# Prologue loads, joint transposes and split order of a two-layer trunk kernel

## The chip, the core and the metric

The kernel runs on one NeuronCore of a Trainium2 chip. The metric is device time per execution in microseconds (us): before the change the median of three runs was 945.95 us (945.51 to 946.14). Five engines work beside each other, each through its own instructions in order: TensorE (PE; its weight loads are listed apart as PEld), VectorE (DVE), ScalarE (ACT), GpSimd (POOL) and SyncE (SP, here only a queue that issues DMAs). An instruction that waits holds up all that stand behind it on its engine.

## The reference, cut to what matters

Two layers run over 256 tokens of width 1024. Each layer is a feed-forward half-step, a mixer with three kinds of heads, and a second feed-forward half-step, and each of the three is set between two RMS norms:

```
for l in range(DEPTH):                                  # DEPTH = 2
    f = swiglu(rmsnorm(h, pre1[l]), wg1[l], wu1[l], wd1[l]);  h = h + 0.5 * rmsnorm(f, post1[l])
    m = mixer(rmsnorm(h, premx[l]), w_in[l], ..., w_out[l]);  h = h + rmsnorm(m, postm[l])
    f = swiglu(rmsnorm(h, pre2[l]), wg2[l], wu2[l], wd2[l]);  h = h + 0.5 * rmsnorm(f, post2[l])

rmsnorm(x, g) = x * rsqrt(mean(x * x) + 1e-6) * g
swiglu(h, wg, wu, wd) = (silu(h @ wg) * (h @ wu)) @ wd      # 1024 -> 2816 -> 1024
```

The mixer projects the normed tokens by `w_in` (q, k, v, z, and the inputs of a state-space scan, a pooling and an attention), and `w_out` brings the heads' outputs back to width 1024.

## The kernel before, in words

**Tokens and weights.** The 256 tokens are two tiles of 128 (t = 0, 1). All weights, some 180 MB, pass through the core once. They come in units of 1 MB (128 partitions by 2048 floats) into four buffers `raw` (L72, on SP's queue), and each is split for the matmuls into a rounded part `hi` (ACT, L103) and the remainder `lo` (DVE, L104), in two or four pieces; five such pairs can be held (SPLIT_BUFS). A product is then three passes on PE: x_hi by w_hi, x_hi by w_lo, x_lo by w_hi. `W.pump` (L115) loads and splits as far ahead as the buffers allow, at the place in the program where it is called.

**One sub-layer's entrance.** `square_sum` (ACT, L226) makes the sums of squares of the two halves of a token tile, `rsqrt_sum` adds eps on DVE (L215), the second sum on ACT (L218) and takes the power -1/2 on POOL (L220); DVE scales the tile (L252) into `n` (the normed tile, two halves). `pre_turn` (L255) then transposes the eight 128x128 blocks on PE (L261) into two PSUM banks, and `split_into` writes them as `xT` hi (ACT, L209) and lo (DVE, L210). After a sub-layer `post` (L229) does the same with the output norm and adds to `h`.

**First products.** `ffn_first` (L397) makes the first 512 columns of gate and up for tile t by `mm_half` (L315, matmul line L324): two weight units for the gate bank, two for the up bank, 12 matmuls each; then `gate` applies silu (ACT, L392) and multiplies (DVE, L394). For t = 0 this stands first, then the transposes of tile 1 (`turned()`), then t = 1. The mixer's `first` (L566) does likewise with q and dt (L313, 24 matmuls of 264 columns) and with k and v.

**Quads and pairs.** Columns of the feed-forward come in groups. A pair (`ffn_pair`, L416) is plain. A quad (`ffn_quad`, L439) multiplies two tiles by two column groups with seven products in place of eight: left factors S1 to S4 are sums and differences of `xT` blocks (L276 to L293), right factors T1 to T4 are sums of weight units made on DVE in place (L102), and one unit is added from memory by an accumulating DMA that POOL issues (L108) after the second piece of T1. Between the products stand the down projections of the columns before (`mm_rows`, L341), for which `turn_h` (L406) transposes the hidden tile (L410) and splits it (L209, L210).

**Order.** A scheduler orders the instructions of each engine at build time, by the order of the code and by `tc.issue_after(ins)`, which keeps what a block issues behind `ins` on that engine. The prologue stands at L941 to L960; `later()` (L964) loads the constants and gains after the first quad.

## Time and profile before

| what | value |
|---|---|
| median of three runs | 945.95 us |
| profiled execution | 946.24 us, of which the span of the trace is 944.5 us |
| PE busy | 927.3 us (98%) |
| DVE busy | 789.1 us (84%) |
| ACT busy | 580.8 us (61%) |
| POOL busy | 34.9 us (4%) |
| DMA | 190.56 MB, mean 202 GB/s |

All times inside the trace count from the start of the span. "Busy" of PE is a sum over pipelined matmuls whose ends are modelled, so the gaps in which PE had nothing to start are read from the idle time that a row gives in brackets and from the distance between the starts of rows.

### The profile page before, as it was taken

The numbers are of one execution on the slowest core, as the hardware profiler recorded it, in microseconds if no ns is written. First come the engines' busy times: TensorE is split into PE (matmuls) and PEld (weight loads), VectorE is DVE, ScalarE is ACT, GpSimd is POOL, SyncE is SP. The second block draws the span as 40 slices with busy tenths as digits, with TensorE's granted clock in tenths as the row PEclk, the third lists the DMA queues.
The fourth block names the chain that finished last, engine by engine and source line by source line (L and its number), as shares of the span: only waits on it lengthen the run. The fifth ranks groups of instructions, "written<-read, shape, count | busy, mean of one in ns | idle before, by whom it ended". The sixth has DMA issues, their size and how long they took to land.

```text
span 944.5 us, 13133 instructions
## 1 busy us (share of the span) xinstructions
PE 927.3 (98%) x5058; PEld 792.5 (84%) x5058; DVE 789.1 (84%) x1067; ACT 580.8 (61%) x923; POOL 34.9 (4%) x47
## 2 busy tenths in 40 slices
PE   7999999999999999999999999999999999999997
PEld 4779898989888789898887888898898887989895
DVE  5899898589887998989499989876888799989872
ACT  5666656468737575747467656556694566656651
POOL 1000000010001000000010000000000010000000
PEclk9999999999999999999999999999999999999999
DMA  8757767555343476758463958583833263858531
GB/s 318 224 216 264 263 182 279 213 190 212 134 149 136 135 272 210 284 148 297 173 196 116 352 143 307 146 318 117 275 128 134 90 201 122 329 180 281 177 116 45
DMA packets 28004, 190.56 MB, mean 202 GB/s; under 512 B 3107, under 2 KB 3363, under 8 KB 5925
## 3 DMA queue, kind: packets, MB, share of 16 engines
q1 hardware_dynamic: 25920, 176.34, 51.0%
q0 software_dynamic: 1728, 12.58, 7.3%
q8 instruction: 40, 0.66, 0.3%
q10 hardware_dynamic: 292, 0.79, 0.2%
q14 instruction: 24, 0.19, 0.1%
HBM read 188.65 MB, written 1.05 MB: 201 GB/s over the span
## 4 chain that ended last, share of the span: by engine, by line
PE 85%; DVE 6%; ACT 5%; issue 2%; DMA 2%; POOL 0%; DVEq 0%; POOLq 0%; ACTq 0%
PE acc L341 26%; PE wk L435 22%; PE wk L305 21%; PE wk L324 10%; DVE lo L104 3%; ACT hi L103 3%; PE wk L410 1%; ACT n L226 1%; DMA raw<-in_ff_q 1%; DVE raw L102 1%; PE wk L873 1%; PE wk L261 1%; DMA n<-in_gains 1%; ACT xT L209 1%; POOL s L220 0%
## 5 line engine op out<-in xcount | busy, mean ns | idle before, releaser
L104 DVE TENSOR_TENSOR lo<-raw,hi 128x1024 fp32r<-128x1024 f32 (+2 forms) x440 | 468.1, 1101 | 58.5 <-ACT hi L103 57.5
L103 ACT ACTIVATE hi<-raw 128x1024 fp32r<-128x1024 f32 (+2 forms) x440 | 400.0, 959 | 167.3 <-DVE raw L102 45.4
L341 PE MATMUL acc<-hi,t 128*128 128x512 f32 x832 | 219.9, 394 | 1.8 <-ACT t L209 1.3
L341 PEld LDWEIGHTS acc<-hi,t 128*128 128x128 f32 x832 | 153.1, 188 | 36.4 <-ACT t L209 5.0
L305 PE MATMUL wk<-xT,hi 128*128 128x256 f32 x1088 | 143.5, 284 | 0.0
L305 PEld LDWEIGHTS wk<-xT,hi 128*128 128x128 f32 x1088 | 136.6, 191 | 1.6
L341 PE MATMUL acc<-lo,t 128*128 128x512 f32 x416 | 114.5, 390 | 0.0
L435 PE MATMUL wk<-hi,n 128*128 128x512 f32 x384 | 102.6, 390 | 1.2 <-DVE t L210 1.2
L324 PE MATMUL wk<-hi,xT 128*128 128x512 f32 x384 | 101.1, 396 | 1.8 <-ACT xT L209 1.0
L341 PEld LDWEIGHTS acc<-lo,t 128*128 128x128 f32 x416 | 78.1, 188 | 16.5
L102 DVE TENSOR_TENSOR raw<-raw,raw 128x1024 f32<-128x1024 f32 x72 | 86.1, 1216 | 3.4 <-DMA raw<-in_ff_q 3.4
L324 PEld LDWEIGHTS wk<-hi,xT 128*128 128x128 f32 x384 | 71.1, 189 | 18.9 <-ACT hi L103 2.2
L435 PEld LDWEIGHTS wk<-hi,n 128*128 128x128 f32 x384 | 71.8, 188 | 17.2 <-issue 2.4
L435 PE MATMUL wk<-hi,xT 128*128 128x512 f32 x288 | 77.8, 392 | 0.0
L305 PE MATMUL wk<-xT,lo 128*128 128x256 f32 x544 | 76.8, 283 | 0.0
L305 PEld LDWEIGHTS wk<-xT,lo 128*128 128x128 f32 x544 | 70.3, 192 | 0.0
L435 PEld LDWEIGHTS wk<-hi,xT 128*128 128x128 f32 x288 | 53.6, 188 | 11.5 <-DVE t L466 0.7
L209 ACT ACTIVATE t<-wk 128x256 fp32r<-128x256 f32 x72 | 26.8, 375 | 43.3 <-DVE t L210 22.1
L324 PE MATMUL wk<-lo,xT 128*128 128x512 f32 x192 | 52.6, 393 | 0.1
L435 PE MATMUL wk<-lo,n 128*128 128x512 f32 x192 | 51.5, 389 | 0.0
L234 DVE TENSOR_TENSOR n<-acc,gains 128x512 f32<-128x512 f32 x24 | 16.5, 687 | 35.8 <-ACT n L226 35.8
L324 PEld LDWEIGHTS wk<-lo,xT 128*128 128x128 f32 x192 | 35.9, 188 | 8.6 <-DVE lo L104 1.0
(172 smaller groups left out, 764.8 us busy)
## 6 DMA issues: line engine op xcount, KB each, us to landing
raw<-in_ff_q SPq DMA_DIRECT2D x48, 1024.0 KB, 5.0
raw<-in_ff_d SPq DMA_DIRECT2D x44, 1024.0 KB, 5.0
raw<-in_ff_f SPq DMA_DIRECT2D x16, 1024.0 KB, 6.0
raw<-in_ff_q POOLq DMA_DIRECT2D x12, 1024.0 KB, 8.0
raw<-in_ff_g SPq DMA_DIRECT2D x12, 1024.0 KB, 4.8
raw<-in_ff_u SPq DMA_DIRECT2D x12, 1024.0 KB, 4.9
raw<-in_w_in SPq DMA_DIRECT2D x10, 1024.0 KB, 4.9
raw<-in_w_kvz SPq DMA_DIRECT2D x8, 1024.0 KB, 5.2
```

The source lines that it names most:

```text
L102: nc.vector.tensor_tensor(raw[:, s], self.raw[x][:, s], self.raw[y][:, s], op=op)
L103: self.act = nc.scalar.activation(hi[:, s], raw[:, s], AF.Copy)
L104: nc.vector.tensor_tensor(lo[:, s], raw[:, s], hi[:, s].bitcast(F32), op=ALU.subtract)
L209: split_into.last = nc.scalar.activation(hi, src_f32, AF.Copy)
L226: nc.scalar.activation(junk, x, AF.Square, scale=1.0 / (gain * math.sqrt(n)), accum_out=ssq)
L234: nc.vector.tensor_tensor(fg[i], f[i], gains[:, 1, i * 512 : (i + 1) * 512], op=ALU.mult)
L261: nc.tensor.transpose(ps[:, k * P : (k + 1) * P], xn[i][:, k * P : (k + 1) * P], ident)
L305: nc.tensor.matmul(ps, w[:, k, s], y[:, k, :], start=i == 0 and k == 0, stop=i == 2 and k == KD - 1)
L324: m = nc.tensor.matmul(ps, y[:, k, :], w[:, k, :], start=h == 0 and n == 0, stop=h == 1 and n == len(parts) - 1)
L341: nc.tensor.matmul(acc[b], x[:, j, s], w[:, j, b * 512 : (b + 1) * 512], start=first and j == 0 and i == 0, stop=last and j == 1 and i == 2)
L410: nc.tensor.transpose(ps[:, k * P : (k + 1) * P], hf[:, k * P : (k + 1) * P], ident)
L435: nc.tensor.matmul(ps, x[:, k, :], w[:, k, :], start=first and n == 0, stop=n == len(parts) - 1, skip_group_check=not first)
```

## The change

**Prologue.** The first token tile and the two gain rows are issued on SP's queue ahead of the weights, not on ACT's queue beside them; the first weight unit comes in two transfers of half its size, and two of its four pieces are split before the transposes, not one. The copies of tile 0 that the quads need (`keep`) stand later on ACT. The constants, gains and the mixer's small parameters are loaded after the first pair, not the first quad, and the three casts of constants follow the splits of that place.

**Norms.** eps is added on POOL (L215 before, L219 after). In `post` both squares stand ahead of the scaled copies.

**Entrances.** `mm_half` takes an `ahead`, which it calls in the second weight unit before the last four of its twelve matmuls. The transposes of tile 1 stand there, in `ffn_first(0)` and in the mixer's `first(0)`, and no longer behind the whole product. Silu of the gate bank is issued as soon as that bank is done. In the program's first feed-forward the factors S1 and S2 (`middle`) are made after the products of `ffn_first(1)` and one further weight split, elsewhere straight after `ffn_first(0)`; the rest of the factors stands behind the splits of `turn_h`; the first weight unit of the first quad, and the mixer's second one (C), are split in four pieces; `pump` calls at the entrances hold one pair fewer and stand behind named instructions.

```diff
...
-    def pump(self):
+    def pump(self, most=SPLIT_BUFS):
...
                 self.load()
-            elif self.split < len(self.jobs) and self.held < SPLIT_BUFS and self.ready():
+            elif self.split < len(self.jobs) and self.held < most and self.ready():
                 self.split_next()
...
     h = consts.tile([P, NT, D], F32, name="h")
-    nc.scalar.dma_start(h[:, 0, :], a["x"][:P, :])
+    nc.sync.dma_start(h[:, 0, :], a["x"][:P, :])
     grow = [buf(tag="n"), buf(tag="n")]
...
         nc.vector.memset(grow[i], 0.0)
-        nc.scalar.dma_start(grow[i][:1], a["gains"][0, 0:1, i * 512 : (i + 1) * 512])
+        nc.sync.dma_start(grow[i][:1], a["gains"][0, 0:1, i * 512 : (i + 1) * 512])
     cst = consts.tile([P, C_ALL], F32, name="cst")
...
+    def cast_constants():
         nc.scalar.activation(after_r, after, AF.Copy)
...
         split_into.last = nc.scalar.activation(hi, src_f32, AF.Copy)
-        nc.vector.tensor_tensor(lo, src_f32, hi.bitcast(F32), op=ALU.subtract)
+        split_into.lower = nc.vector.tensor_tensor(lo, src_f32, hi.bitcast(F32), op=ALU.subtract)
...
         v, r = tiny(1), tiny(1)
-        nc.vector.tensor_scalar(v, ssq[0], eps, None, op0=ALU.add)
+        nc.gpsimd.tensor_scalar(v, ssq[0], eps, None, op0=ALU.add)
         for s in ssq[1:]:
             w = tiny(1)
-            nc.scalar.activation(w, s, AF.Identity, bias=v)
+            rsqrt_sum.last = nc.scalar.activation(w, s, AF.Identity, bias=v)
             v = w
...
+    def pump_behind(ins):
+        with tc.issue_after(ins.ins):
+            W.pump()
...
-        ssq = [square_sum(f[0], D, gain)]
+        ssq = [square_sum(f[i], D, gain) for i in range(2)]
+        r = rsqrt_sum(ssq, EPS / (gain * gain))
         scaled(0)
-        ssq.append(square_sum(f[1], D, gain))
-        r = rsqrt_sum(ssq, EPS / (gain * gain))
         scaled(1)
...
+        def middle():
+            part("S1", s1)
+            nc.vector.tensor_tensor(x11, s1, x11, op=ALU.subtract)
+            part("S2", x11)
...
         nc.vector.tensor_tensor(s1, turned[0], s1, op=ALU.subtract)
-        part("S1", s1)
         nc.vector.tensor_tensor(s3, x11, turned[0], op=ALU.subtract)
-        nc.vector.tensor_tensor(x11, s1, x11, op=ALU.subtract)
-        part("S2", x11)
-        left["rest"] = rest
+        left["middle"], left["rest"] = middle, rest
         for i, (name, k, t_) in enumerate((("X11", 0, 0), ("X12", 4, 0), ("X22", 4, 1))):
...
             for n, (k, i) in enumerate(parts):
+                if ahead and h == 1 and n == 8:
+                    ahead()
                 y, w = ((x[0], hi), (x[0], lo), (x[1], hi))[i]
...
                 g1, u1, u2 = (W.unit(src[k]) for k in (0, 1, 3))
-                p["g1", i] = W.job(g1)
+                p["g1", i] = W.job(g1, pieces=2 if i > QUADS[0] else 4)
                 p["T1", i] = W.job(g1, (g1, ALU.add, u1), then=(u1, src[3]))
...
-    def gate(pg, pu):
-        s = buf()
-        nc.scalar.activation(s, pg, AF.Silu)
+    def gate(pg, pu, s=None):
+        if s is None:
+            s = buf()
+            nc.scalar.activation(s, pg, AF.Silu)
         hf = buf()
...
-    def ffn_first(t, p, pin=False):
+    def ffn_first(t, p, pin=False, ahead=None, between=None):
...
         for i in range(2):
-            mm_half(ps[i], [p["f", i, k] for k in range(2)], t, pin)
-        hf = gate(*ps)
-        W.pump()
+            mm_half(ps[i], [p["f", i, k] for k in range(2)], t, pin, ahead if i else None)
+            if not i:
+                s = buf()
+                nc.scalar.activation(s, ps[0], AF.Silu)
+        hf = gate(*ps, s)
+        with tc.issue_after(pre_turn.lower.ins):
+            if between:
+                W.split_next()
+                between()
+            W.pump(SPLIT_BUFS - t)
         return hf
...
         turn(1)
-        W.pump()
         if "rest" in left:
-            left.pop("rest")()
+            with tc.issue_after(split_into.last.ins):
+                left.pop("rest")()
+                W.pump()
+        else:
+            W.pump()
         pb = bank()
...
         hT = {}
-        hf = [ffn_first(0, p, pin=later is not None)]
-        turned()
-        hf.append(ffn_first(1, p))
+        hf = [ffn_first(0, p, later is not None, turned)]
+        middle = left.pop("middle")
+        if later is None:
+            middle()
+        hf.append(ffn_first(1, p, between=middle if later else None))
...
                 before = [i, i + 1]
-            if later:
+            if later and i in PAIRS:
                 later()
...
         post(1, acc[1], gain)
+        summed = rsqrt_sum.last
         xn1 = before_next(1)
-        W.pump()
-        return lambda: pre_turn(1, xn1, left=next_left)
+        W.pump(SPLIT_BUFS - 1)
+        def turn_second():
+            pre_turn(1, xn1, left=next_left)
+            pump_behind(split_into.last)
+        if next_left is not None:
+            pump_behind(summed)
+            return lambda: pre_turn(1, xn1, left=next_left)
+        return turn_second
...
         for i, k in enumerate(("B", "C", "x0", "x1", "u")):
-            p[k] = W.plan(a["w_in"][l, i], pieces=2 if i else 4)
+            p[k] = W.plan(a["w_in"][l, i], pieces=2 if i > 1 else 4)
         for k in range(2):
...
-    def mixer(l, p, turned, next_left, before_next):
+    params = {}
+    def load_params(l):
         vec = small.tile([P, V_ALL], F32, tag="vec", name=f"vec{l}", bufs=1)
...
         nc.sync.dma_start(row, a["row"][l : l + 1, :].to_broadcast([P, R_ALL]))
+        return vec, row
+    def mixer(l, p, turned, next_left, before_next):
+        vec, row = params.pop(l) if l in params else load_params(l)
...
-        def first(t):
+        def first(t, ahead=None):
             pq, pkv = bank(), bank()
...
             last and W.done(p["q"])
-            mm_half(pkv, [p["kv", k] for k in range(2)], t)
             c = buf()
...
             nc.vector.tensor_tensor(dtr[:, t, :], pq[:, 256:QDT], row[:, R_DTB : R_DTB + HEADS], op=ALU.add)
+            mm_half(pkv, [p["kv", k] for k in range(2)], t, ahead=ahead)
             nc.scalar.activation(c[:, 256:], pkv[:, :256], AF.Copy)
...
-        first(0)
-        turned()
+        first(0, turned)
         first(1)
...
     left = {}
-    W.split_next((0,))
+    W.split_next((0, 1))
     keep = pre_turn(0, xn0, left=left, late=True)
     with tc.issue_after(split_into.last.ins):
-        W.split_next((1, 2, 3))
+        W.split_next((2, 3))
         W.load()
...
     with tc.issue_after(W.act.ins):
-        keep()
         W.split_next()
...
         xn1 = pre_scale(1, gain)
-        W.pump()
+        keep()
+        W.pump(SPLIT_BUFS - 1)
...
     def later():
-        more_constants()
-        load_gain(1, 0, 1)
-        load_gain(0, 0, 2)
+        with tc.issue_after(W.dma.ins):
+            more_constants()
+            load_gain(1, 0, 1)
+            load_gain(0, 0, 2)
+            params[0] = load_params(0)
+        with tc.issue_after(W.act.ins):
+            cast_constants()
...
```

The first place is SP's queue at the program's start; `h` is the token tile, `n` the two gain rows, `raw` the weight units. Before:

```order
L1086 UNCONDITIONAL_BRANCH
L78 DMA raw_105<-in_ff_f 128x2048
L78 DMA raw_107<-in_ff_f 128x2048
L942 DMA h<-in_x 128x1024
L78 DMA raw_154<-in_ff_f 128x2048
L78 DMA raw_156<-in_ff_f 128x2048
```

and after the change:

```order
L1132 UNCONDITIONAL_BRANCH
L166 DMA h<-in_x 128x1024
L170 DMA n_75<-in_gains 1x512
L170 DMA n_76<-in_gains 1x512
L78 DMA raw_105<-in_ff_f 128x1024 x2
L78 DMA raw_108<-in_ff_f 128x2048
L984 DMA h<-in_x 128x1024
L78 DMA raw_155<-in_ff_f 128x2048
L78 DMA raw_157<-in_ff_f 128x2048
```

Three small issues now stand ahead of the first weights on SP, and the first unit is two issues.

The second place is ACT in the first quad. `t_391` (after: `t_388`) and `t_393` (`t_390`) are the transposed hidden tile, from PE's banks `wk_395` and `wk_434` (`wk_392`, `wk_431`); `raw_200` (`raw_201`) is the unit to which the accumulating DMA (DMASW0) adds; names in square brackets are the semaphores an instruction waits for. Before:

```order
L103 ACTIVATE hi_375<-raw_214 128x1024
L209 ACTIVATE t_391<-wk_395 128x2x128 [waits PE_49]
L103 ACTIVATE hi_383<-raw_200 128x1024 [waits DMASW0_49,Activation_49]
L103 ACTIVATE hi_367<-raw_198 128x1024 [waits DVE_49]
L103 ACTIVATE hi_383<-raw_200 128x1024
L209 ACTIVATE t_391<-wk_434 128x2x128 [waits PE_49]
L209 ACTIVATE t_393<-wk_395 128x2x128 [waits DVE_49]
```

and after the change:

```order
L103 ACTIVATE hi_372<-raw_199 128x1024 [waits DVE_49]
L213 ACTIVATE t_388<-wk_431 128x2x128 [waits PE_49]
L213 ACTIVATE t_390<-wk_392 128x2x128 [waits DVE_49]
L213 ACTIVATE t_390<-wk_431 128x2x128 [waits DVE_49]
L213 ACTIVATE n_440<-t_280 128x512
L468 ACTIVATE t_414<-wk_401 128x512
L472 ACTIVATE t_429<-wk_416 128x512
L213 ACTIVATE n_445<-t_197 128x512 [waits DVE_49]
L103 ACTIVATE hi_449<-raw_201 128x1024 [waits DMASW0_49,Activation_49]
```

The split that waits for the accumulating DMA stood ahead of three of the four copies of the hidden tile; now it stands behind all four.

The third place is PE at the entrance of the first layer's second feed-forward; `n_2855`, `n_2856` (after: `n_2864`, `n_2865`) are the halves of the normed tile 1, and `hi`, `lo` the weight units. Before:

```order
L324 MATMUL wk_2904<-lo_2886,xT_103 128x512 x4
L324 MATMUL wk_2904<-hi_2885,xT_104 128x512 x4
L261 MATMUL wk_2957<-ident,n_2855 128x128 x4
L261 MATMUL wk_2964<-ident,n_2856 128x128 x4
L324 MATMUL wk_2985<-hi_2607,xT_103 128x512 x4
```

and after the change:

```order
L336 MATMUL wk_2917<-lo_2895,xT_103 128x512 x4
L268 MATMUL wk_2964<-ident,n_2864 128x128 x4
L268 MATMUL wk_2971<-ident,n_2865 128x128 x4
L336 MATMUL wk_2917<-hi_2894,xT_104 128x512 x4
L336 MATMUL wk_2998<-hi_2616,xT_103 128x512 x4
```

Four matmuls that stood ahead of the eight transposes now stand between them and the first product of tile 1, which reads what ACT makes of the transposes.

## Rows read from the trace of the kernel before

**Rows 1.** The page: engines over the span, and the chain that ended last.

```profile
PE 927.3 (98%) x5058; PEld 792.5 (84%) x5058; DVE 789.1 (84%) x1067; ACT 580.8 (61%) x923; POOL 34.9 (4%) x47
...
PE 85%; DVE 6%; ACT 5%; issue 2%; DMA 2%; POOL 0%; DVEq 0%; POOLq 0%; ACTq 0%
```

**Rows 2.** Timeline 0 to 17 us: start, us, engine, line, tile [idle before, releaser].

```profile
0.79 0.41 ACTq L165 DMA_DIRECT2D h<-in_x  x1
...
7.30 0.63 ACT L226 ACTIVATE n<-h 128x512 bf16<-128x512 f32 x1 [3.73 <-DMA h<-in_x]
...
7.64 3.75 PE L945 MATMUL acc<-n,n 128*128 128x512 f32 x4 [2.57 <-DMA n<-in_gains]
...
9.49 0.80 POOL L220 TENSOR_TENSOR s<-s,halfexp 128x1 f32<-128x1 f32 x1 [8.13 <-ACT s L218]
...
11.18 2.17 PE L261 MATMUL wk<-ident,n 128*128 128x128 f32 x8
...
13.00 0.78 PE L324 MATMUL wk<-hi,xT 128*128 128x512 f32 x1
...
14.55 1.54 PE L324 MATMUL wk<-hi,xT 128*128 128x512 f32 x3 [0.78 <-ACT hi L103]
```

**Rows 3.** DMA issues of the first 20 us: count, KB each, median us to landing.

```profile
raw<-in_ff_f SPq DMA_DIRECT2D x4, 1024.0 KB, 9.7
...
h<-in_x ACTq DMA_DIRECT2D x1, 512.0 KB, 6.5
```

**Rows 4.** DMA issues of the whole span: a transfer with the queues empty.

```profile
out<-h SPq DMA_DIRECT2D x3, 256.0 KB, 2.1
```

**Rows 5.** Timeline 26 to 40 us: ACT at tile 1, and the end of the first products.

```profile
26.08 1.28 ACT L392 ACT_TABLE_LOAD   x1
...
27.87 1.08 ACT L209 ACTIVATE xT<-wk 128x512 fp32r<-128x512 f32 x2
...
39.55 0.60 PE L410 MATMUL wk<-ident,t 128*128 128x128 f32 x4
...
39.91 1.17 PE L435 MATMUL wk<-hi,xT 128*128 128x512 f32 x4
```

**Rows 6.** The chain of waits, 35 to 48 us: start, us, what.

```profile
35.79 1.14 DVE raw L102
...
37.25 8.60 DMA raw<-in_ff_q
...
45.94 2.02 ACT hi L103 x2
```

**Rows 7.** Timeline 49 to 54 us: PE in the first quad.

```profile
49.21 1.21 PE L341 MATMUL acc<-hi,t 128*128 128x512 f32 x4 [1.27 <-ACT t L209]
...
51.86 1.88 PE L341 MATMUL acc<-hi,t 128*128 128x512 f32 x7 [0.52 <-DVE t L210]
```

**Rows 8.** Stretch: us, busy (count) of PE, PEld, DVE, ACT, POOL, clock, DMA share, GB/s.

```profile
54.00:200.00 146.00, 145.97 (x801) 127.06 (x801) 124.84 (x143) 92.01 (x128) 3.18 (x4) 1.00 0.66 228
```

**Rows 9.** Timeline 205 to 212 us: entrance of the first mixer.

```profile
205.38 1.41 DVE L252 SCALAR_TENSOR_TENSOR n<-h,s,gains 128x512 f32<-128x512 f32 x2 [0.44 <-POOL s L220]
...
206.81 1.04 PE L261 MATMUL wk<-ident,n 128*128 128x128 f32 x8
...
208.21 1.25 PE L313 MATMUL wk<-hi,xT 128*128 128x264 f32 x8 [0.36 <-ACT xT L209]
...
210.33 1.63 PE L313 MATMUL wk<-hi,xT 128*128 128x264 f32 x8
```

**Rows 10.** Timeline 305 to 331 us: entrance of the first layer's second feed-forward.

```profile
305.72 1.42 DVE L252 SCALAR_TENSOR_TENSOR n<-h,s,gains 128x512 f32<-128x512 f32 x2 [0.44 <-POOL s L220]
...
308.54 1.03 PE L261 MATMUL wk<-ident,n 128*128 128x128 f32 x8
...
309.83 1.19 PE L324 MATMUL wk<-hi,xT 128*128 128x512 f32 x4 [0.25 <-ACT xT L209]
...
330.57 1.17 PE L435 MATMUL wk<-hi,n 128*128 128x512 f32 x4 [0.39 <-DVE t L210]
```

**Rows 11.** Line L220 over the span: count: min/median/max ns, first and last start.

```profile
L220 POOL TENSOR_TENSOR s<-s,halfexp x28: 547/870/1437, 9.5 to 939.5; 128x1 f32<-128x1 f32 x28
```

More of the change, by code (lines that the diff above doesn't have):

```diff
@@ L77, in load @@
         for c in range(0, cols, step):
-            self.nc.sync.dma_start(t[:, c : c + step], src[:, c : c + step])
+            self.dma = self.nc.sync.dma_start(t[:, c : c + step], src[:, c : c + step])
         self.raw[i] = t
@@ L263, in pre_turn @@
             split_into(xT, at, ps.rearrange("p (k n) -> p k n", k=4))
+            pre_turn.lower = split_into.lower
             turned.append(ps)
@@ L313, in mm_tok, with mm_half @@
                 nc.tensor.matmul(ps, x[:, k, s], w[:, k, :], start=i == 0 and k == 0, stop=i == 2 and k == KD - 1)
-    def mm_half(ps, us, t, pin=False):
+    def mm_half(ps, us, t, pin=False, ahead=None):
         for h, u in enumerate(us):
@@ L931, in mixer @@
         post(1, acc[1], 1.0)
+        summed = rsqrt_sum.last
         xn1 = before_next(1)
-        W.pump()
+        W.pump(SPLIT_BUFS - 1)
+        pump_behind(summed)
         return lambda: pre_turn(1, xn1, left=next_left)
@@ L938, in hybrid_trunk_kernel @@
         plans.append((plan_ffn(l, 1), plan_mix(l), plan_ffn(l, 2)))
-    W.load()
+    W.load(2)
     W.load()
@@ L959, in hybrid_trunk_kernel @@
         xn1 = pre_scale(1, gain)
-        W.pump()
+        keep()
+        W.pump(SPLIT_BUFS - 1)
     turned = lambda: pre_turn(1, xn1, left=left)
     def later():
-        more_constants()
-        load_gain(1, 0, 1)
-        load_gain(0, 0, 2)
+        with tc.issue_after(W.dma.ins):
[5 more added lines that the diff above has]
+            cast_constants()
     for l in range(DEPTH):
```

## The prediction

> **What bounds the kernel now.** I read the page first. PE is busy 98% of the span and holds 85% of the chain that ended last [rows 1], so only time in which PE has nothing to start can be won. The stretches say where that is: from 54 to 200 us PE is busy 145.97 of 146 us, with the clock granted in full [rows 8]; the gaps lie in the first 54 us and at the five later entrances of a sub-layer. The timeline shows each gap's releaser. The profiled execution took 946.24 us, 1.7 us of it outside the span; I make the sum against it and take 0.3 us off at the end, since the median is 945.95.
>
> *Prologue.* PE's first product of weights starts at 13.00 [rows 2]. Back from there: transposes at 11.18, the power on POOL at 9.49, the first square at 7.30, and that one waited for the token tile, which ACT issued at 0.79 [rows 2] and which landed 6.5 us later, while the weight units beside it took 9.7 us [rows 3].
>
> *First products.* Three further matmuls wait for ACT's split, to 14.55 [rows 2]. At tile 1 ACT loads a table (1.28 us) and then writes xT, at 27.87 [rows 5]. The products end at 39.55.
>
> *First quad.* PE waits 1.27 us for a copy of the hidden tile on ACT and 0.52 us for its remainder on DVE [rows 7]. The chain shows why: the accumulating DMA ran from 37.25 to 45.85, and ACT's split that needs it (45.94) stands ahead of the copy [rows 6].
>
> *Entrances.* In the mixer the eight transposes start at 206.81 and the next product at 208.21 [rows 9]; in the feed-forward at 308.54 and 309.83 [rows 10]. Four transposes unhindered take 0.36 us from start to start (39.55 to 39.91) [rows 5], so eight take 0.72: the mixer loses 0.68 us, the feed-forward 0.57. The mixer's third pass (x_lo) takes 1.63 us against 1.25 for eight like it, 0.38 more [rows 9]; the quad loses 0.39 us at 330.57 [rows 10]. There are two mixers, and three feed-forwards beside the first, each like the one shown.
>
> **The change part by part.**
>
> *Loads in one queue.* Before, 512 KB of tokens shared the engines with the weights. Now they go first. Nearest rows: 256 KB through an empty queue landed 2.1 us after issue [rows 4]. Twice the bytes can take at most twice that, 4.2, and the part that does not grow with the bytes is in it once: I take 3.3 us, between the two, landing at 4.1 instead of 7.3. Bounds: 2.1 (half the size) and 6.5 (as now), that is a gain of 4.4 to 0 us. The chain behind it keeps its length except for two things: two splits (0.6 us each) stand on ACT ahead of the second sum, not one, +0.6; and the gain rows, which PE's broadcast product needs, come on the same queue ahead of the weights, so that product (3.75 us [rows 2], started at 7.64) moves up too. Against +0.6 stands the second scaled half, which before waited for that product. Gain 3.0 us. The price: three issues of some 0.4 us stand ahead of the first weights on SP, and two of them wait for memsets of VectorE, so every weight unit starts up to 1.6 us later. ACT did not reach the fourth unit's split until long after its landing, which hides that; uncovered it would cost 1.6 us.
>
> *Two pieces split early, later copies.* The wait of 14.55 less 13.00 less a matmul goes in part: two matmuls now have their weights, the third and fourth wait for splits behind xT. Of some 1.1 us I take 0.7; the saved copies and the silu ahead of its turn on ACT give 0.5 more at tile 1. Gain 1.2 us, bounds 0 and 2.5 (what these products lose beyond 96 unhindered matmuls, after the 1.1, is no more). What is late next is DVE's splits of the first quad.
>
> *First quad.* The copies now stand ahead of the split that waits for the DMA, and the constants (five transfers, 2 MB) no longer run in this stretch. Both sums of T1 come before the next factor on DVE, so the accumulation starts earlier. I take 1.27 + 0.52 = 1.8, and 0.2 for short waits beside them: gain 2.0 us. DVE then has ten splits and sums of 1.14 us, the first of [rows 6], between T1 and the hidden tile; by my sequence of its instructions the tile's remainder is ready about when PE asks. If it is late by one of them the gain is 0.8; bounds 0 and 2.5.
>
> *Constants after the first pair.* Nothing reads them before the first mixer or the output norm; the five transfers move past some twelve weight loads on SP. PE did not wait once from 54 to 200 [rows 8]: nothing.
>
> *Transposes ahead of the last four matmuls.* Four matmuls of 0.23 us cover ACT's two copies (0.6 us each) almost wholly. In the feed-forward the normed tile is ready at 305.72 + 1.42 = 307.14 and the transposes would stand at 308.54 - 0.91 = 307.63 [rows 10]: ready by 0.5 us, gain 0.57 of 0.57. In the mixer it is ready at 206.79 [rows 9] and the transposes would stand at 205.90, so PE waits 0.9 us, less what the shorter norm chain saves. In the old order ACT has a split between the last sum of `post` and its addition (1.0 us each, by the two of [rows 6]), and the new order has the addition on POOL instead: about 0.8. Then 0.1 to 0.2 is left. Gain 0.5 of 0.68, and 0.3 of the 0.38, since xT's remainder is made sooner too: 0.8 a mixer, bounds -0.3 and 1.2. For the feed-forwards I add half of the quad's 0.39 and 0.1 of small waits: 0.85 each, bounds 0 and 1.5.
>
> *eps on POOL.* 28 additions leave DVE, where a row stood in a queue behind other work. The power on POOL took 0.55 to 1.44 us [rows 11]; an addition of one column is not shown there. From above it is bounded by the slowest of these, 1.44, from below by nothing. I take 0.55, the power's fastest. With two sums the addition runs beside the second square (0.63 us [rows 2]) and costs nothing; four single sums in the mixers pay about 0.4 us each where the state-space result is not waited for. If the cover is gone, see the slower rival.
>
> *Four pieces for the first quad's unit and for C, fewer pairs held, silu with its bank.* Twelve splits become 24 of half size, under 0.1 us each on ACT and DVE, hidden by PE; one pair fewer held matters only where splits run just ahead of PE. Nothing.
>
> *Tail.* The last tile's chain has the same steps in the same order: nothing.
>
> Sum: 3.0 + 1.2 + 2.0 + 2 x 0.8 + 3 x 0.85 = 10.35 us. 946.24 - 10.35 = 935.9, and with the 0.3 us to the median 935.6; I round to **936**.
>
> One rule speaks against the addition on POOL. The slowest powers (1.44 us) come while DVE subtracts two SBUF tiles, the fastest (0.55) at the very end where DVE is idle [rows 11]. The Trainium skill ("SBUF — State Buffer", Who interferes with whom) says that a VectorE instruction with two SBUF inputs and a GpSimd instruction that reads SBUF exclude each other, and whichever comes second waits. By that rule, the trace agrees: 0.55 against 1.44.
>
> **Rivals.**
>
> *A: the entrances give nothing.* The normed tile is late and PE waits in front of the transposes as long as it waited behind them. For it: 0.9 us in the mixer. Against: 0.5 us to spare in the feed-forward. 945.95 - 6.2 = 939.8.
>
> *B: the start gives only the token tile's 3 us.* DVE's sums and splits set the first quad, so PE arrives early and waits. For it: DVE was busy 84% [rows 1] and the splits of the first quad were finished within a few us of their use. Against: ACT's split there waited for a DMA of 8.60 us [rows 6], which none of DVE's work did. 945.95 - 3.0 - 4.15 = 938.8.
>
> *C: hardly anything.* Weights bound the start, the token tile gains nothing, and the entrances fall short: 945 to 947. For it: the same bytes pass the same 16 engines. Against: no row of the start waits for a first weight unit.
>
> *D: slower, by the addition on POOL.* Each entrance has two roots in line on tile 1 (output norm, then input norm). If each addition waits for a DVE operation on two SBUF tiles of 1.14 us [rows 6] and then runs 0.87 (the power's median [rows 11]), it ends 2.0 us after the first sum, 1.4 us later than the second square (0.63): ten of them, 14 us, less 1.5 us to spare in three feed-forwards, and the entrances' gain is gone. 945.95 - 6.2 + 12.5 = 952.3, or 953.7 with one more at the start. It makes the kernel slower once an addition ends more than about 0.8 us after the second square, at 1.4 us length. Against: DVE's pieces at the entrances are mostly half size.
>
> **How the numbers follow.** My forecast 0.55; A 0.13; B 0.13; C 0.11; D 0.08. The forecast's own range from its terms is 932.5 to 938.5: the better bounds are 1.4 + 1.3 + 0.5 + 0.8 + 1.95 beyond the sum, of which I allow a bit over half together. A and B lie inside 942.5; C and D stay out. Range **932.5 to 942.5**. A measurement of this kernel tells no change from a change beyond about 0.2%, 1.9 us: faster is the forecast, A, B and a sliver of C and D, 0.85; within it the bulk of C, 0.08; slower most of D, 0.07.
>
> **What would show it.** Right: the first square near 4.1 us and the first weight product near 10; the product's end near 35; no wait of PE above 0.5 us in the first quad; transposes and next products at the entrances without an idle of PE between; the pair's first product some 6 us earlier than before. Wrong: a first square past 6; PE waiting for DVE's `lo` around 40 to 60 us; idle time of PE in front of the transposes; additions on POOL over a microsecond with the scalar addition on ACT behind them.

## The result and the profile after

The changed kernel takes 937.51 us (median of 5 runs, 937.19 to 937.75) where the kernel before takes 945.95 (945.51 to 946.14): ratio 0.9911, 95% interval 0.9896 to 0.9925. The profiled spans are 935.5 and 944.5 us. The page answers to [rows 1]: PE's busy time fell from 927.3 to 921.8 (waits hidden in stretched matmuls went), and PE's share of the chain rose from 85 to 94%.

```profile
PE 921.8 (99%) x5058; PEld 792.9 (85%) x5058; DVE 788.1 (84%) x1051; ACT 580.4 (62%) x935; POOL 41.4 (4%) x75
...
PE 94%; DVE 2%; ACT 1%; POOL 1%; issue 1%; DMA 1%; POOLq 0%; DVEq 0%; SPq 0%; ACTq 0%
```

Where the 9.0 us of span came from is read by comparing the start of the same PE instruction in both traces:

| PE instruction | before | after | gain so far |
|---|---|---|---|
| first product of weights | 13.00 | 12.47 | 0.53 |
| first transposes of a hidden tile (end of the first products) | 39.55 | 37.41 | 2.14 |
| transposes in the first pair (behind the first quad) | 78.60 | 74.06 | 4.54 |
| hidden tile, second feed-forward | 321.00 | 315.35 | 5.65 |
| hidden tile, third | 501.81 | 494.79 | 7.02 |
| hidden tile, fourth | 781.84 | 773.00 | 8.84 |

To give each place its own share I add up, over both traces, how much later each matmul's successor starts than at the unhindered pace (0.227 us for 512 columns, 0.121 for 264), and call it PE's loss; it counts equal work, whatever its order. By that: up to the first product 0.53, first products 1.61, first quad 2.40, mixers 0.52 each, later feed-forwards 1.35, 1.29 and 1.39 (entrance and quad), tail -0.54, the rest -0.07.

The start differs from one profile to the next. Four of the kernels below start in the same order as the changed kernel (old pumps, old order in the quad, constants early, eps on VectorE but not at the start). In these five profiles the first product comes at 11.55 to 12.51 and the first products end at 37.07 to 37.69, so one profile does not tell a difference below 1 us in the one, or below 0.6 us in the other, from chance.

The start is the surprise. The timeline of the changed kernel, 0 to 17 us (columns as in [rows 2]):

```profile
0.80 0.39 SPq L166 DMA_DIRECT2D h<-in_x  x1
...
4.29 0.63 ACT L234 ACTIVATE n<-h 128x512 bf16<-128x512 f32 x1 [2.22 <-DMA h<-in_x]
...
7.91 1.15 ACT L103 ACTIVATE hi<-raw 128x512 fp32r<-128x512 f32 x2 [2.29 <-DMA raw<-in_ff_f]
...
8.96 0.28 ACT L222 ACTIVATE s<-s,s 128x1 f32<-128x1 f32 x1
...
11.13 1.31 PE L268 MATMUL wk<-ident,n 128*128 128x128 f32 x8 [3.95 <-DVE n L259]
...
12.47 2.48 PE L336 MATMUL wk<-hi,xT 128*128 128x512 f32 x4
```

The square moved up by 3.01 us, where 3.2 were forecast. But the two early splits now stand ahead of the addition of the second sum (L222), and they wait 2.29 us for the first weights. The addition runs at 8.96 though its operands were there at 5.6.

In the first quad PE waits for nothing. The same stretch of the changed kernel, then of the kernel before (columns as in [rows 8]):

```profile
37.00:74.00 37.00, 37.00 (x191) 31.59 (x190) 35.71 (x40) 26.15 (x33) 0.00 (x0) 1.00 0.69 239
```

```profile
37.00:74.00 37.00, 35.21 (x162) 28.63 (x162) 33.98 (x37) 24.25 (x31) 1.03 (x1) 1.00 0.65 202
```

The mixer's entrance after, 197 to 207 us; it answers to [rows 9]:

```profile
197.96 1.90 DVE L104 TENSOR_TENSOR lo<-raw,hi 128x512 fp32r<-128x512 f32 x3
...
198.30 1.64 POOL L219 TENSOR_SCALAR s<-s 128x1 f32<-128x1 f32 x1 [2.24 <-ACT n L234]
...
199.97 0.30 ACT L222 ACTIVATE s<-s,s 128x1 f32<-128x1 f32 x1 [0.95 <-POOL s L219]
...
201.84 1.29 PE L268 MATMUL wk<-ident,n 128*128 128x128 f32 x8 [0.27 <-DVE n L259]
...
202.89 1.17 PE L336 MATMUL wk<-hi,xT 128*128 128x512 f32 x4
...
205.83 1.13 PE L323 MATMUL wk<-hi,xT 128*128 128x264 f32 x8
```

The wait behind the transposes is gone, and about as long a one (0.70 us of loss, 0.27 of it shown as idle, the rest in the modelled end of the matmul before and in the transposes, which take 1.29 us instead of 1.03) stands in front of them: the normed tile is late because the eps addition on POOL lasted 1.64 us, until VectorE's three splits were through. What the mixer does gain is the third pass, 1.13 us for eight where it was 1.63 [rows 9].

The feed-forward's entrance, 299 to 306 us, against [rows 10]: the normed tile is early, and no idle time is left.

```profile
299.22 1.42 DVE L259 SCALAR_TENSOR_TENSOR n<-h,s,gains 128x512 f32<-128x512 f32 x2 [0.46 <-POOL s L224]
...
302.67 1.03 PE L268 MATMUL wk<-ident,n 128*128 128x128 f32 x8
...
303.46 2.07 PE L336 MATMUL wk<-hi,xT 128*128 128x512 f32 x8
```

The new operation over the whole span (count: shortest/median/longest in ns):

```profile
L219 POOL TENSOR_SCALAR s<-s x28: 219/222/1637, 5.1 to 928.4; 128x1 f32<-128x1 f32 x28
```

### The profile page after: what moved, and what is told of

Its sections match the earlier page's. It is cut to its first block, busy times and chain, and to the rows that moved or that the text cites. A ratio compares the mean times of both kernels' runs of the same rounds, so it can differ in the third digit from the quotient of the medians.

```text
span 935.5 us, 13148 instructions
## 1 busy us (share of the span) xinstructions
PE 921.8 (99%) x5058; PEld 792.9 (85%) x5058; DVE 788.1 (84%) x1051; ACT 580.4 (62%) x935; POOL 41.4 (4%) x75
## 4 chain that ended last, share of the span: by engine, by line
PE 94%; DVE 2%; ACT 1%; POOL 1%; issue 1%; DMA 1%; POOLq 0%; DVEq 0%; SPq 0%; ACTq 0%
PE acc L353 29%; PE wk L456 25%; PE wk L315 21%; PE wk L336 13%; PE wk L431 1%; PE wk L268 1%; DVE lo L104 1%; PE wk L913 1%; PE wk L323 1%; DMA raw<-in_ff_f 1%; ACT n L234 0%; PE acc L665 0%; DVE n L259 0%; POOL s L224 0%; POOL s L219 0%
## 5 line engine op out<-in xcount | busy, mean ns | idle before, releaser
L456 PEld LDWEIGHTS wk<-hi,n 128*128 128x128 f32 x384 | 71.9, 188 | 15.9 <-issue 1.1
L242 DVE TENSOR_TENSOR n<-acc,gains 128x512 f32<-128x512 f32 x24 | 16.1, 690 | 35.3 <-ACT n L234 35.3
```

The source lines that it names most:

```text
L242: nc.vector.tensor_tensor(fg[i], f[i], gains[:, 1, i * 512 : (i + 1) * 512], op=ALU.mult)
L456: nc.tensor.matmul(ps, x[:, k, :], w[:, k, :], start=first and n == 0, stop=n == len(parts) - 1, skip_group_check=not first)
```

## The experiments

Twelve kernels, each timed four or five times. The kernel before, timed beside them on four occasions, had medians of 945.96 to 946.33, so a difference of 0.4 us between kernels timed on different occasions is at the edge of what the times tell. Unless said otherwise an edit is to the changed kernel (937.51).

**Norm first.** The two splits of the start go behind the addition.

```diff
-    W.split_next((0, 1))
+    with tc.issue_after(rsqrt_sum.last.ins):
+        W.split_next((0, 1))
```

> Changed kernel with one order: at the start ACT adds the second sum (L222) ahead of the first two weight splits (L103), not behind them. My theory: the start gained 0.66 us instead of 3.0 because those two splits waited 2.29 us for the first weights and took 1.05, in front of the addition that the norm waits for. Then the first product of weights starts near 10.0 instead of 12.47 and the kernel takes 935.5 us (934.5 to 936.5; the changed kernel 937.5). Rival: the first weights, landed near 7.9, and their splits bound the start anyway; then the first product moves up, the next products wait for splits as much longer, and the time stays at 937.0 to 937.7.

937.00 us (936.69 to 937.18). The first product came at 9.44, but the hidden tile's first transposes only at 36.94 against 37.41. The timeline shows where 3 us became 0.5: ACT waits for the third unit, then PE for the fourth unit's split and for tile 1's copies.

```profile
9.44 0.73 PE L336 MATMUL wk<-hi,xT 128*128 128x512 f32 x2
...
15.69 2.19 ACT L103 ACTIVATE hi<-raw 128x512 fp32r<-128x512 f32 x4 [1.54 <-DMA raw<-in_ff_f]
...
21.36 0.30 PE L268 MATMUL wk<-ident,n 128*128 128x128 f32 x1 [1.02 <-ACT hi L103]
...
24.14 1.08 ACT L213 ACTIVATE xT<-wk 128x512 fp32r<-128x512 f32 x2
...
24.79 0.73 PE L336 MATMUL wk<-hi,xT 128*128 128x512 f32 x2 [0.56 <-ACT xT L213]
```

In the changed kernel these copies of tile 1 stand at nearly the same time, though its first product starts 3.03 us later:

```profile
24.60 1.08 ACT L213 ACTIVATE xT<-wk 128x512 fp32r<-128x512 f32 x2
```

In nine of the thirteen kernels with the change the first products end 12.79 to 12.86 us after these copies start, whether the first product comes at 9.44 or at 12.51; in the other four it is 11.66 to 13.52. So ACT's way to these copies sets that end, not the first product. My theory held for the first product and fell for the time: that is the rival's (937.0 to 937.7).

**Token tile on ACT's queue**, in the changed kernel and in the one with the norm first.

```diff
-    nc.sync.dma_start(h[:, 0, :], a["x"][:P, :])
+    nc.scalar.dma_start(h[:, 0, :], a["x"][:P, :])
...
-        nc.sync.dma_start(grow[i][:1], ...)
+        nc.scalar.dma_start(grow[i][:1], ...)
...
```

> Changed kernel with the token tile and the gain rows on ACT's queue again, all else kept. My theory: as long as ACT's splits stand ahead of the addition, the first weights set the start and the token tile's place is worth little: first product of weights 12.3 to 13.5, 937.5 to 938.5 us. Rival, as predicted before: the token tile's place is worth 3 us, so 940 to 941.

> The kernel with the norm first (937.0), with the token tile and gain rows on ACT's queue again. My theory: the weights bound the first products, so the token tile's place moves the first product of weights by 2 to 3 us, from 9.44 to about 12, but not the time: 937.0 to 937.9. Rival: the token tile's place is worth the predicted 3 us once the splits are out of the norm's way: 939.5 to 940.

937.92 (937.72 to 937.98) and 937.99 (937.69 to 938.33). In the first the square starts at 6.56 instead of 4.29, and the addition at 8.84, no later than in the changed kernel: 2.3 us that nothing uses. In the second the first product starts at 11.20, 1.76 later, and the first products end at 36.89, where they ended at 36.94 with the token tile first. What this edit costs (0.4 and 1.0 us) lies elsewhere, in part in a wait of PE near 57.5 us for a split (0.41 and 0.28 us of idle shown); the rest, and its way there, I did not follow. The first time is my theory's; the second is 0.1 us beyond it and far from the rival's 3 us.

**Second token tile behind the fourth weight unit**, with the norm first.

```diff
-    nc.sync.dma_start(h[:, 1, :], a["x"][P:, :])
...
         W.load()
         W.load()
+        nc.sync.dma_start(h[:, 1, :], a["x"][P:, :])
         W.split_next()
```

> The kernel with the norm first (its time was 937.0), and the second token tile's load moved from between the second and third weight unit to behind the fourth. My theory: with the norm early the arrival of the four weight units bounds the first products (ACT waited 0.86 and 1.54 us for the second and third unit there); 512 KB less ahead of the third and fourth unit brings them some 1.2 us earlier, and the kernel takes 936.2 us (935.7 to 936.7). Rival: ACT's own order bounds them (norm of tile 1, the kept copies and a table load stand around the fourth unit's splits); then the time stays at 936.8 or rises to 938 because tile 1's normed tile comes late.

939.38 (938.97 to 939.64): slower than either expectation. ACT's wait for the third unit fell from 1.54 to 0.27 us, as my theory has it, but the fourth unit's splits now came behind two kept copies and a table load, and tile 1's norm behind them.

```profile
15.00 2.20 ACT L103 ACTIVATE hi<-raw 128x512 fp32r<-128x512 f32 x4 [0.27 <-DMA raw<-in_ff_f]
...
20.64 1.54 PE L336 MATMUL wk<-hi,xT 128*128 128x512 f32 x3 [0.73 <-ACT hi L103]
...
23.42 0.50 PE L336 MATMUL wk<-hi,xT 128*128 128x512 f32 x1 [1.24 <-ACT hi L103]
```

So both count: the third unit's landing, and ACT's order behind it.

**Silu's table first**, on the kernel with eps on VectorE (below).

```diff
+    early = consts.tile([P, 1], F32, name="early")
+    nc.scalar.activation(early, halfexp, AF.Silu)
```

> The kernel with eps on VectorE (935.54), and a Silu of one column as ACT's first instruction, so that the table that holds Silu is the one loaded at the start and the second load (1.28 us, at 22.16, ahead of the copies of tile 1's transposed norm) goes. My theory: the first products end near 37 us in every version (losses up to there 11.0 to 11.7 us, whether the first product starts at 9.4 or 12.5) because ACT is busy without a gap from the third unit's landing (15.5) to tile 1's copies (23.95); 1.28 us less there starts tile 1's first product as much earlier: 934.4 us (934.1 to 934.8). Rival: the weights' arrival or VectorE sets that end, and the time stays at 935.3 to 935.8.

935.20 (935.10 to 935.44), 0.3 less than without, which is at the edge of what the times tell; my 934.4 was missed. From the third unit's first split to tile 1's copies ACT took 23.26 - 16.22 = 7.04 us instead of 23.95 - 15.49 = 8.46; the load is gone, and no other came in its place. But the third unit's first split came 0.73 us later in this run and took half of it back. The last experiment follows from that.

**Second token tile between the third and fourth unit**, on that kernel: its load moves one place.

```diff
-    nc.sync.dma_start(h[:, 1, :], a["x"][P:, :])
...
         W.load()
+        nc.sync.dma_start(h[:, 1, :], a["x"][P:, :])
         W.load()
```

> The fastest kernel so far (eps on VectorE, Silu's table first: 935.20), with the second token tile's load moved one place: behind the third weight unit, ahead of the fourth (behind the second before). The table experiment saved 1.4 us between the third unit's first split and tile 1's copies, but the third unit landed 0.73 us later in it. My theory: the third unit's arrival (16.22 there, ACT waited 1.53 for it) now sets the chain; 512 KB less ahead of it brings it near 15.0, the norm of tile 1 does not wait for its tokens, and the time is 934.2 us (933.8 to 934.7). Rival: tile 1's tokens, landing 2.4 us later, then hold up its norm, or the fourth unit comes late: 935.0 to 936.

933.87 (933.64 to 934.52), ratio 0.9867 (0.9851 to 0.9884): the fastest of all, 3.6 us under the changed kernel. My theory held. ACT splits the rest of the first three units in one go, without a wait, as in the changed kernel, but from 12.12 (12.97 there), and the second table load is gone too: tile 1's copies come at 22.37 (24.60), and the first products end at 35.89 (37.41).

```profile
12.12 5.31 ACT L103 ACTIVATE hi<-raw 128x512 fp32r<-128x512 f32 x10
...
22.37 1.07 ACT L215 ACTIVATE xT<-wk 128x512 fp32r<-128x512 f32 x2
```

**eps on VectorE**, everywhere, and everywhere but at the start.

```diff
-        nc.gpsimd.tensor_scalar(v, ssq[0], eps, None, op0=ALU.add)
+        nc.vector.tensor_scalar(v, ssq[0], eps, None, op0=ALU.add)
```

> Changed kernel with the addition of eps on VectorE again. The order of the code then also has ACT's addition ahead of the two splits at the start, as in the run with the norm first, so this one is read against that run. My theory: GpSimd's addition costs only where it ran into VectorE's splits, 1.64 us instead of 0.22 at the two mixers: this kernel is 0.3 to 1.5 us faster than the run with the norm first, and the wait in front of the mixer's transposes (0.27 us) goes. Rival: on VectorE the addition stands in a queue behind splits again and each entrance loses 0.3 us or more: 1.5 us or more slower than the run with the norm first.

> Changed kernel with eps on VectorE everywhere but in the two norms at the start, so that the start keeps its order. My theory: GpSimd's addition costs 0.55 us at each mixer, where it lasts 1.64 us beside VectorE's splits, and nothing elsewhere: 936.4 us (936.0 to 936.7). Rival: the 1.5 us between the kernel with eps on VectorE and the one with the norm first came from the start's other order; then 937.2 to 937.7.

935.54 (935.36 to 936.18) and 936.38 (935.77 to 937.02). In both the addition takes 0.15 us between two splits, and the loss in front of the mixers' transposes falls from 0.70 and 0.73 to 0.11 and 0.18 us (second kernel 0.12 and 0.20); other places keep theirs. Mixer entrance with eps on VectorE:

```profile
197.99 0.14 DVE L219 TENSOR_SCALAR s<-s 128x1 f32<-128x1 f32 x1
...
200.84 1.13 PE L268 MATMUL wk<-ident,n 128*128 128x128 f32 x8
```

So the addition on POOL costs 1.1 us in two places out of 28. The other 0.8 us of the first kernel lies at the start: its first products end at 36.77, those of the second kernel at 37.69. There eps on VectorE also puts the second sum's addition ahead of the splits; the engine, that order and chance are not told apart.

**Old pumps.** More pairs held, no `pump` behind the sum or behind the transposes' split, C's unit in two pieces.

```diff
-        W.pump(SPLIT_BUFS - 1)
+        W.pump()
...
-            pump_behind(summed)
...
```

> Changed kernel with the pumps at the end of a sub-layer as before (no pair less held, none behind the sum's addition or behind the turn's last copy) and C's unit split in two pieces again. My theory: VectorE's splits of 1024 columns come between the normed tile and the remainder of xT again, so the mixer's third pass loses part of the 0.5 us that each mixer gained: 938.5 us (938.0 to 939.2). Rival: the copies of the first bank, which the change emits ahead of the second products, moved the remainder up, and the pumps change nothing: 937.2 to 937.8.

939.75 (939.19 to 940.50), slower than expected and for another reason. The third pass keeps its 1.13 us. The loss in front of the mixers' transposes grows to 1.83 and 1.86 us, since the eps addition starts 0.31 us later, behind one more split of VectorE, and lasts 2.17 us, 0.53 longer. It again meets a run of three splits and ends 0.08 us after it; the third now has 1024 columns and takes 1.22 us instead of 0.69 (the row names the shape of the first):

```profile
198.27 2.43 DVE L104 TENSOR_TENSOR lo<-raw,hi 128x512 fp32r<-128x512 f32 x3
...
198.61 2.17 POOL L219 TENSOR_SCALAR s<-s 128x1 f32<-128x1 f32 x1 [2.10 <-ACT n L234]
...
202.69 1.29 PE L268 MATMUL wk<-ident,n 128*128 128x128 f32 x8 [1.40 <-DVE n L259]
```

So the pumps and C's four pieces, which I had priced at nothing, are worth 1.13 us a mixer as long as eps is added on POOL; which of the three parts of this edit does it was not tried.

**Transposes behind.**

```diff
-                if ahead and h == 1 and n == 8:
-                    ahead()
...
+        if ahead:
+            ahead()
```

> Changed kernel with the transposes of tile 1 behind tile 0's last four matmuls again, all else kept. The five later entrances gained 5.1 us in all (0.5 at each mixer, 1.3 to 1.4 at each feed-forward). My theory: the place of the transposes is most of that: 941.3 us (940.5 to 942.5), with waits of PE of 0.3 to 0.7 us behind the transposes again. Rival: the shorter norm chain and the later split copies made the gain, and the place of the transposes little: 937.5 to 939.

938.99 (938.43 to 940.24). The loss returns at the three feed-forwards, 0.53, 0.54 and 0.53 us, with the wait that [rows 10] shows:

```profile
303.69 1.03 PE L268 MATMUL wk<-ident,n 128*128 128x128 f32 x8
...
304.98 1.19 PE L334 MATMUL wk<-hi,xT 128*128 128x512 f32 x4 [0.25 <-ACT xT L213]
```

At the mixers it only changes side (0.67 behind, 0.70 in front). The waits are my theory's, the time is the rival's (937.5 to 939): the place is worth 1.5 to 1.6 us, not 4.

**Old order in the quad**: no pump behind the transposes' split, the tile differences split at once, the rest of the factors not held behind `turn_h`'s splits.

```diff
-        with tc.issue_after(pre_turn.lower.ins):
-            if between:
-                W.split_next()
-                between()
-            W.pump(SPLIT_BUFS - t)
+        if between:
+            between()
+        W.pump()
...
```

> Changed kernel with the old order of splits and copies behind tile 1's first products and in the first quad of each feed-forward (no pump behind the transposes' split, the differences of the tile split at once); constants stay late. My theory: this order is what won 2.4 us in the first quad and about 0.6 us in the quad of each later feed-forward (losses of 0.69 to 0.89 us before, 0.25 to 0.28 after): 941.0 us (940.0 to 942.0). Rival: the constants made the first quad's gain; then only the later quads lose: 938.5 to 939.5.

941.63 (941.29 to 942.16). The quads of the later feed-forwards lose 0.85, 1.30 and 0.85 us again instead of 0.25 to 0.28. The first quad loses 0.83, and the stretch from the pair to the first mixer 0.8 more. So the time is my theory's, but the shares are not: of the first quad's 2.4 us only 0.83 comes back. ACT's rows, of the kernel before and then of this one, show what is missing:

```profile
45.94 2.95 ACT L103 ACTIVATE hi<-raw 128x1024 fp32r<-128x1024 f32 x3 [4.02 <-DMA raw<-in_ff_q]
```

```profile
39.44 5.88 ACT L103 ACTIVATE hi<-raw 128x1024 fp32r<-128x1024 f32 x6 [1.35 <-DVE raw L102]
...
45.23 0.64 ACT L213 ACTIVATE t<-wk 128x256 fp32r<-128x256 f32 x2
```

Here, too, the split that waits for the accumulating transfer (the fifth of the six, at 43.31) stands ahead of three of the four copies. But the transfer was issued at 35.13 (37.25 before, 33.44 in the changed kernel), ACT had other splits to do until it landed, and it waited for nothing where it waited 4.02 us before. The order of copies and splits alone is worth 0.83 us; no run shows which part of the change brought the other 1.6.

**Constants early**, the five transfers and three casts behind the first quad's code as before, parameters at the mixer.

```diff
-            if later and i in PAIRS:
+            if later:
...
```

> Changed kernel with the constants, gains and their casts issued behind the first quad's code again, as before, and the two parameter loads at the first mixer. My theory: the five transfers share the engines with the accumulating transfer of the first quad, which took 8.60 us before; PE waits again in the first quad: 938.5 us (938.0 to 939.5). Rival: the order of copies and splits on ACT made that gain alone: 937.2 to 937.8.

937.65 (936.86 to 938.16): no change. PE is busy 37.00 of 37 us there too, and the accumulating transfer lands in 8.1 us, against 8.0 without the constants and 8.60 before [rows 6]. The constants are still under way in its first 2.0 us: the last of them whose landing is recorded lands 8.6 us after 26.67, at 35.3, and the accumulating transfer is issued at 33.29. In the kernel before that was 1.4 us (9.3 after 29.32, and 37.25). The first line is of this run, the second of the kernel before (columns as in [rows 3]):

```profile
vec<-in_vec SPq DMA_DIRECT2D x1, 149.0 KB, 8.6
```

```profile
row<-in_row SPq DMA_DIRECT2D x1, 268.0 KB, 9.3
```

So in the new order the constants cost nothing. Early constants together with the old order were not run.

## Why the prediction was right, point by point

The time lies 1.5 us above the 936.0 forecast, inside the range and inside the forecast's own. The sum was nearly right because errors cancel: the token tile gave 2.5 us less than forecast, each mixer 0.3 less and the tail 0.5 less; the feed-forwards together gave 1.5 more, the first products and the first quad 0.4 more each. That they cancel to within 1.4 us is luck. Of the signs that the prediction named, the first square (4.29) and the quiet first quad came. The first product "near 10" (12.47), the products' end "near 35" (37.41) and the pair "some 6 us earlier" (4.54) did not, and two of its signs of being wrong showed at the mixers: idle time of PE in front of the transposes (0.27 us) and an addition on POOL over a microsecond.

- **Token tile first: wrong, 3.0 forecast, 0.5 measured** (0.5 to 1.5 over the five profiles with this start). The landing came as said (square at 4.29, 4.1 forecast). The step that failed is "the chain behind it keeps its length except for two things: two splits (0.6 us each)". I priced the splits by their duration and not by what they wait for: the first half of their unit landed at 7.9, and the addition stood behind them. The same part had the price of this, weights that start "up to 1.6 us later", and called it hidden, by looking at the fourth unit: the first unit's issue moved from 0.79 to 2.29, and ACT waited 2.29 us for it. The norm-first run shows a second cover below: with the first product at 9.44 the first products still end only 0.5 us earlier, less than the spread of the start, because the third unit's landing and ACT's unbroken work up to tile 1's copies set that end. TensorE's lower clock at the start (last section) is not what held it: the norm-first run and the one with the token tile on ACT's queue have the full clock from 9 to 19 us (1.00) and end at 36.94 and 37.28. The last start experiment shows it from the other side. Rival C had this in its one line, that weights bound the start.
- **First products: right, 1.2 forecast, 1.6 measured.** It does not need the token tile first: with the tile on ACT's queue the hidden tile's transposes start at 37.28, no later than in the changed kernel. Which of its parts gave it no run separates; the transposes' place is not one of them (37.49 with the transposes behind).
- **First quad: right, 2.0 and 2.4.** PE waits nowhere in it. The constants cost nothing in the new order. The old order, put back, costs 0.83 of the 2.4; the rest may lie in ACT's wait of 4.02 us for the accumulating transfer, which is now issued 3.81 us earlier, but no run shows that part alone. B's late remainder did not come.
- **Mixers: direction right, 0.8 each forecast, 0.5 measured, by another path.** Of the 0.5 I gave to the transposes nothing came: the normed tile is as late in front as xT was behind. The third pass gave 0.5 against 0.3 said. That the copies of the first bank, emitted earlier, cause it is read from the order and supported by the pump run; it was not tried alone. The transposes' place is not the cause: with the transposes behind, that pass takes 1.13 us as well.
- **Feed-forwards: mis-sized, 0.85 each and 1.35 measured.** The transposes' 0.57 was 0.53 (eight unhindered ones take 0.79 us from start to next product, 302.67 to 303.46, not 0.72). The quad's remainder gave 0.6, not half of 0.39, since the loss also sits in stretched matmuls that show no idle time; small waits make up the rest.
- **eps on POOL: 0 forecast, 1.1 us lost.** "With two sums the addition runs beside the second square (0.63 us [rows 2]) and costs nothing" holds but for two of 28 places: at the other 26, four of them single sums, the addition takes 0.22 to 0.93 us, and at the entrances no wait of PE goes with it. At the two mixers the mechanism of rival D is real: 1.64 us. D was wrong in how often it happens. The Trainium skill ("SBUF — State Buffer", Who interferes with whom) says that a VectorE instruction with two SBUF inputs and a GpSimd instruction that reads SBUF exclude each other. By that rule, the trace agrees: 1.64 us against 0.22, and 2.17 where one of the splits is twice as wide. The prediction misread its own example: beside the fastest power (939.53) VectorE was not idle, it multiplied a PSUM bank by the gains from 939.16 to 939.85, with one input in SBUF.
- **Tail: 0 forecast, 0.5 lost.** 0.1 of it is in the chain; the rest is the last store, issued at 932.11 with the span ending at 935.5, against 941.56 and 944.5 before. That is not chance of one profile: all thirteen kernels with the change have 3.40 or 3.41 us from that store's issue to the end, where the one profile before has 2.97. Why is open.

## What to carry to other kernels

A wait costs everything queued behind it on its engine: when a step moves ahead of a chain, price it by when its input lands, not by how long it runs. Bringing the first product forward was worth at most half a microsecond here, and is worth little until the last thing that the first products need, here the third weight unit and ACT's way to tile 1's copies, comes forward too; so look at the end of a stretch before its beginning. A tiny operation on GpSimd cost time here where it met VectorE in a run of two-input operations on SBUF; at such a place put it on VectorE, between two of them.

## What the runs showed of the hardware

The one-column addition on POOL did not get in between VectorE's splits: issued in the first of three, it ended 0.08 us after the third (199.94 and 199.86).

In the changed kernel TensorE's clock was for a while not at its full level. The engine had nothing to do from 7.2 to 11.13 us and then worked on, and the granted clock was 0.86 and 0.80 of 2.4 GHz in the two stretches from 9 to 19 us: 0.50, the lower of its two levels (1.2 GHz), from 12.6 to 15.9, and full around it; four matmuls at 14.75 took 1.65 us, where four took 1.07 from 18.05 on. The kernel with the norm first, with no such pause, has 1.00 in both. The stretches of the changed kernel:

```profile
9.00:14.00 5.00, 2.83 (x11) 1.57 (x11) 3.82 (x7) 2.36 (x6) 0.96 (x1) 0.86 1.01 419
14.00:19.00 5.00, 5.00 (x19) 3.97 (x19) 5.00 (x9) 5.00 (x12) 0.03 (x1) 0.80 1.02 413
...
12.60:15.90 3.30, 3.29 (x7) 2.06 (x8) 3.30 (x6) 3.30 (x7) 0.00 (x0) 0.50 1.02 433
```
